# Scores from stacked split queries over 128 rows, in a given TensorE order between projection pieces

## The chip, the cores and the metric

The kernel runs on one core of one Trainium2 chip. The metric is the device time of one execution in microseconds (us). A core has a matrix engine (TensorE, PE in the profile), a vector engine (VectorE, DVE), a scalar engine for activations and copies (ScalarE, ACT), a general engine (GpSimd, POOL) and SyncE (SP), which issues transfers; DMAs can also be issued from ACT's queue. The engines run beside each other and wait for one another by semaphores. On-chip memory is SBUF, and TensorE writes its sums to PSUM.

## What is computed

Two layers of a decoder on 512 tokens of 1024 channels, in float32. Layer 0 is attention, layer 1 is RWKV-7; each is followed by a squared-ReLU MLP of width 4096. The change lies in layer 0:

```python
def hybrid_attention(h, w_in, w_out, lam_p, subln, lam_init):
    proj = h @ w_in
    aq, ak, av, bq, bk, bv = jnp.split(proj, cuts, axis=-1)      # 512 columns each
    aq = partial_rope(heads(aq, A_HEADS), pos) * scale           # 8 heads of 64
    ak = partial_rope(heads(ak, A_HEADS), pos)
    oa = mixture_of_dilations(aq, ak, heads(av, A_HEADS))        # mixer A
    ...
    bq = partial_rope(two_maps(bq), pos) * scale                 # 4 heads, 2 maps of 64
    bk = partial_rope(two_maps(bk), pos)
    lam = jnp.exp(jnp.sum(lp[0] * lp[1])) - jnp.exp(jnp.sum(lp[2] * lp[3])) + lam_init
    ob = differential_attention(bq, bk, heads(bv, B_HEADS), lam, subln, lam_init)
    return jnp.concatenate([oa, ob], axis=-1) @ w_out
```

Mixer A mixes three causal, dilated windows by their softmax denominators, which is one softmax with the logarithm of how often each key occurs added to its score. Mixer B is `(softmax(s0) - lam * softmax(s1)) @ v` for two maps of each head, then an RMS norm over the head's 128 outputs.

## The kernel before

**Products.** A product with a weight matrix is made in three single-pass products (type float32r) of parts that have been split into a high and a low part: high by high, high by low, low by high (`mm3`, lines 174 to 178). `wchunk` loads two blocks of 128 weight rows by 512 columns (`wraw`, from SP), ACT casts the high part (`whi`), VectorE subtracts for the low part (`wlo`). `gemm_group` runs a product over four PSUM banks: for each chunk of two blocks, four banks `m` by two blocks `k`, three products each. Activations are split in the same way (`xh`, `xl`; `oh`, `ol` for the attention's outputs; `split`).

**Attention.** The order in the code is: values `va`, queries `qa`, keys `ka`, mixer A (`attend_a`), then `qb`, `kb`, `vb`, then mixer B (`attend_b`), then the output product with `Wo` (two halves of 512 input rows, two column groups), whose evacuation adds to the residual `h`. `project_qk` evacuates each block of 128 channels so: ACT copies it (`qraw`), VectorE multiplies it by the cosine, four DMAs on ACT's queue swap the rotated channels (`sw`), POOL multiplies these by the sine (`rt`), and VectorE adds. Queries use tables with the factor -0.125 in them (`cosq`, `sinq`).

Scores are one float32 product over the 64 rows of a head, 128 queries by `n` keys (`n` is 128, 256, 384 or 512 by query block `i`; the trace shows two instructions for each). Two heads (mixer A) or two maps (mixer B) lie in the two halves of the 128 rows. `probs` then adds the mask table and finds the row minimum on VectorE (`sb`, `mn`), and ACT makes the exp with its row sum. `pv` transposes the result on TensorE (`t`), ACT copies it (`pts`), TensorE multiplies it by the values (`o`). `attend_a` goes over query blocks, in each over eight heads; `attend_b` over query blocks, in each over four heads and two maps, with `w` and the subtraction of the maps on VectorE, then squares (`junk`), a power on POOL (`rs2`) and the scaled output `ob`. `to_channels` transposes an `ob` on TensorE and splits it into `oh`, `ol`.

**Order.** The code's order is not the engines' order: a scheduler in the build places instructions of different steps by its own reckoning, under dependences and free buffers. In attention nothing else fixes the order but a few dependences between value products. So projections of mixer B and the first half of `Wo` fall between steps of the mixers where the scheduler put them. In the RWKV layer the class `InOrder` ties instructions of an engine into the order in which they are written.

Of the kernel before, what the change touches and what calls it, by code (L numbers as in the profile page):

```python
# [10 lines left out]
F32 = mybir.dt.float32  # L11
# [7 lines left out]
P = 128  # L19
S = 512  # L20
# [89 lines left out]
""".split())  # L110
HU = 4
CW = HU * HD

# [31 lines left out]
class Builder:  # L145
# [67 lines left out]


    def build(self):
        tc, nc, A = self.tc, self.nc, self.A
        with ExitStack() as ctx:
# [3 lines left out]
            self.const = pool("const")  # L221
            self.open_w()
# [29 lines left out]
            self.open_h()  # L252

# [9 lines left out]
            self.close_w()  # L263

# [95 lines left out]
    def attention_layer(self):  # L360
        tc, nc, A = self.tc, self.nc, self.A
        with ExitStack() as ctx:
# [10 lines left out]
            cosq, sinq = (ac.tile([P, S], F32, name=n) for n in ("cosq", "sinq"))  # L373
            dl = ac.tile([P, 4 * HD], F32, name="dl")
            sub = ac.tile([P, 1], F32, name="sub")

# [35 lines left out]
            def project_v(c0, name, meanwhile=None, prep=None):  # L412
# [4 lines left out]
                self.gemm_group(W, 0, KT, c0, xh, xl, evac, token_major=True, meanwhile=meanwhile, prep=prep, chunk=prep and chunk)  # L417
                return v
            for k in range(AHEAD):
                channels(k)  # L420
            va = project_v(1024, "a", token_norm, lambda k: k + AHEAD < KT and channels(k + AHEAD))
            xin.release()
            aw = pool("aw", 2)
            prb = self.bcast(r0)
            for t, tq in ((cos, cosq), (sin, sinq)):
                nc.vector.tensor_tensor(t, t, prb, op=ALU.mult)
                nc.gpsimd.tensor_scalar(tq, t, -0.125, None, op0=ALU.mult)
# [6 lines left out]
            def project_qk(c0, name, ct, st):  # L434
                q = ac.tile([P, NB, S], F32, tag="Q" + name, name=self.nm("Q" + name))

                def evac(m, ps):
# [4 lines left out]
                    nc.vector.tensor_tensor(q[:, m, :], ps, ct, op=ALU.mult)  # L442
# [4 lines left out]
                    nc.gpsimd.tensor_tensor(t, sw, st, op=ALU.mult)  # L447
                    nc.vector.tensor_tensor(q[:, m, :], q[:, m, :], t, op=ALU.add)
                self.gemm_group(W, 0, KT, c0, xh, xl, evac)
                return q  # L450

            def probs(q, k, mm_, hh, i, table, total):
# [3 lines left out]
                rows = slice(hh * HD, (hh + 1) * HD)  # L456
                ps = ps_s.tile([P, S], F32, tag="s", name=self.nm("s"))
                nc.tensor.matmul(ps[:, :n], q[rows, mm_, i * P:(i + 1) * P], k[rows, mm_, :n], start=True, stop=True)
# [1128 lines left out]
```

## Time and profile before

| | |
|---|---|
| time, median of 3 runs | 1525.69 us (1523.87 to 1530.07) |
| profiled execution | 1525.81 us, of which its span is 1523.9 |
| TensorE busy | 1443.8 us, 95% |
| VectorE, ACT, POOL busy | 57%, 45%, 23% |
| mean granted TensorE clock | 0.976 of full speed |
| attention from the end of `ka` to the first MLP product | 88.9 to 294.2 us |

The span is the time from the first to the last instruction. A share of busy time is a mean over stages with different limits. TensorE's instructions overlap: one starts before the one ahead of it has ended, so what a product costs is read from one start to the next, not from its own length.

### The profile page before, as it was taken

The page shows a single profiled execution, that of the slowest core. Times are in us where ns is not written, and L with a number is a line of the kernel's source. Part 1 is how long each engine was busy: PE and PEld are TensorE (multiplying, and loading weights), DVE is VectorE, ACT ScalarE, POOL GpSimd, SP SyncE. Part 2 cuts the span into 40 slices and gives each one's busy share as a digit, 9 for nine tenths or more (in the row PEclk, how much of TensorE's full clock was granted, in tenths as well). Part 3 has the DMA queues.
Part 4 walks back from the last instruction along what each step waited for, and adds up shares of the span by engine and source line. Part 5 has one row for each costly group of instructions (what it writes and reads, how often), then busy time and mean ns, then how long its engine had stood idle before and what let it go on. Part 6 is the DMA issues. An engine that isn't in the chain of part 4 may idle for free. (4 is left out here: it accounts for less than half of the span.)

```text
span 1523.9 us, 24386 instructions
## 1 busy us (share of the span) xinstructions
PE 1443.8 (95%) x9506; PEld 1172.4 (77%) x9506; DVE 863.7 (57%) x1491; ACT 684.2 (45%) x1394; POOL 352.0 (23%) x364
## 2 busy tenths in 40 slices
PE   7999999999999999969888999989998999999998
PEld 6765866878888888857667788868787888888887
DVE  5343565632335464497876778878866333354543
ACT  4245364432334343236634666666655233343533
POOL 4210200300000010052336455546655000000100
PEclk9999999999999999979989999989999999999999
DMA  5230310433333233324564345444223333333331
GB/s 193 80 90 1 96 57 27 102 104 85 97 97 97 97 124 98 102 64 152 176 192 147 116 139 154 127 143 119 64 95 118 90 97 97 97 97 97 97 97 70
DMA packets 117115, 159.76 MB, mean 105 GB/s; under 512 B 22524, under 2 KB 57892, under 8 KB 117000
## 3 DMA queue, kind: packets, MB, share of 16 engines
q1 hardware_dynamic: 103240, 140.37, 30.8%
q10 hardware_dynamic: 13760, 17.83, 3.5%
q8 instruction: 75, 1.23, 0.3%
q14 instruction: 40, 0.33, 0.1%
HBM read 133.00 MB, written 19.92 MB: 100 GB/s over the span
## 5 line engine op out<-in xcount | busy, mean ns | idle before, releaser
L169 DVE TENSOR_TENSOR wlo<-wraw,whi 128x1024 fp32r<-128x1024 f32 x172 | 219.9, 1280 | 263.1 <-ACT whi L167 263.0
L167 ACT CAST whi<-wraw 128x1024 fp32r<-128x1024 f32 x172 | 180.5, 1050 | 253.0 <-PE g L177 236.2
L176 PE MATMUL g<-xh,whi 128*128 128x512 f32 x640 | 250.2, 391 | 1.1 <-DVE Qa L442 1.1
L178 PE MATMUL g<-xh,wlo 128*128 128x512 f32 x640 | 249.0, 391 | 1.3 <-DVE wlo L169 1.1
L177 PE MATMUL g<-xl,whi 128*128 128x512 f32 x640 | 249.8, 390 | 0.0
L176 PE MATMUL g<-mh,whi 128*128 128x512 f32 x512 | 199.2, 389 | 0.0
L177 PE MATMUL g<-ml,whi 128*128 128x512 f32 x512 | 199.2, 389 | 0.0
L178 PE MATMUL g<-mh,wlo 128*128 128x512 f32 x512 | 199.2, 389 | 0.0
L316 POOL TENSOR_TENSOR acc<-acc,sq 128x512 f32<-128x512 f32 x29 | 48.8, 1683 | 636.4 <-issue 436.5
L184 DVE TENSOR_TENSOR ml<-m,mh 128x512 fp32r<-128x512 f32 x128 | 90.0, 706 | 148.9 <-ACT mh L183 148.8
L183 ACT CAST mh<-m 128x512 fp32r<-128x512 f32 x128 | 78.7, 616 | 191.3 <-PE g L178 191.1
L178 PEld LDWEIGHTS g<-xh,wlo 128*128 128x128 f32 x640 | 120.1, 188 | 28.3 <-DVE wlo L169 3.0
L176 PEld LDWEIGHTS g<-xh,whi 128*128 128x128 f32 x640 | 120.1, 188 | 27.2 <-DVE Qa L442 1.8
L177 PEld LDWEIGHTS g<-xl,whi 128*128 128x128 f32 x640 | 120.3, 188 | 24.7 <-issue 0.3
L178 PEld LDWEIGHTS g<-mh,wlo 128*128 128x128 f32 x512 | 96.1, 188 | 20.1
L176 PEld LDWEIGHTS g<-mh,whi 128*128 128x128 f32 x512 | 96.1, 188 | 20.1
L177 PEld LDWEIGHTS g<-ml,whi 128*128 128x128 f32 x512 | 96.1, 188 | 19.7
L137 POOL TENSOR_TENSOR wlo<-wraw,whi 128x256 fp32r<-128x256 f32 x100 | 76.6, 770 | 119.3 <-ACT whi L137 115.3
L177 PE MATMUL g<-wlo,xh 128*128 128x512 f32 x160 | 65.3, 408 | 4.5 <-DVE wlo L169 4.5
L176 PE MATMUL g<-whi,xh 128*128 128x512 f32 x160 | 63.0, 408 | 5.8 <-ACT xh L641 4.7
L643 POOL TENSOR_TENSOR xl<-mt,xh 128x512 fp32r<-128x512 f32 x28 | 47.5, 1712 | 86.9 <-ACT xh L641 73.5
L178 PE MATMUL g<-whi,xl 128*128 128x512 f32 x160 | 65.0, 406 | 0.6 <-POOL xl L643 0.5
(313 smaller groups left out, 2757.8 us busy)
## 6 DMA issues: line engine op xcount, KB each, us to landing
wraw<-in_mlp_w_dram SPq DMA_DIRECT2D x128, 512.0 KB
wraw<-in_attn_w_in_dram SPq DMA_DIRECT2D x24, 512.0 KB
wraw<-in_rwkv_w_o_dram SPq DMA_DIRECT2D x16, 512.0 KB
wraw<-in_attn_w_out_dram SPq DMA_DIRECT2D x8, 512.0 KB
wraw<-in_rwkv_w_k_dram SPq DMA_DIRECT2D x8, 512.0 KB
wraw<-in_rwkv_w_r_dram SPq DMA_DIRECT2D x8, 512.0 KB
wraw<-in_rwkv_w_v_dram SPq DMA_DIRECT2D x8, 512.0 KB
xt<-in_x_dram ACTq DMA_DIRECT2D x4, 512.0 KB
```

What stands on the lines that cost most here:

```text
L137: ins = op(*args, **kw)
L167: ins = [nc.scalar.copy(hi, raw)]
L169: ins.append((eng or nc.vector).tensor_tensor(lo, raw, hi, op=ALU.subtract))
L176: mm(ps, lh, rh, start=start, stop=False)
L177: mm(ps, lh, rl, start=False, stop=False)
L178: mm(ps, ll, rh, start=False, stop=stop)
L183: nc.scalar.copy(hi, src)
L184: nc.vector.tensor_tensor(lo, src, hi, op=ALU.subtract)
L316: nc.gpsimd.tensor_tensor(self.acc[0], self.acc[0], sq, op=ALU.add)
L643: eng.tensor_tensor(xl[k], t, xh[k], op=ALU.subtract)
```

## The change

- **Scores.** `stacked` puts the high part of a head's scaled query in its own 64 rows and the low part in the other 64 (type float32r); the key's high part (`kh`) and low part (`kl`) are each copied by a DMA into the other half, so that they stand twice. A score is then two single-pass products over 128 rows, with `kh` and with `kl`, which make all four products of the parts. `cosq` and `sinq` go; the factor -0.125 is in `stacked`.
- **By head pairs.** Mixer A runs over four pairs of heads, in each over two heads and four query blocks (8 slots); mixer B over four heads, in each over four query blocks (4 slots) with both maps. Outputs are normed and turned into channels by pair or head, and `Wo` runs in three parts (rows 0 to 3, 4 to 5, 6 to 7).
- **In a given order.** `at` gives each step a slot: in mixer A a score at slot + 0.6, its transposes at + 1.3, its value product at + 2.0; in mixer B at + 0.6, + 2.2 and + 2.8. `gemm_stream` gives the products of `qb`, `kb`, `vb` and `Wo` in 160 pieces of three products, and `FILL` says how many pieces are issued by which slot. `InOrder` fixes the order on TensorE alone; the other engines keep the scheduler's.
- **Buffers.** `sb` has 6 buffers instead of 4, `ob` 2 instead of 5. Six `fill` tiles of 64 to 224 bytes are written once and never read.

```diff
+FILL = [(-2, 0), (-1, 0), (0, 18), (33, 96), (36, 104), (48, 140), (60, 144)]
...
+            self.edge = self.tc.alloc_tile_pool(name="edge", bufs=1, side="right")
+            self.fill(self.edge, 224)
...
+    def fill(self, pool, size):
+        self.nc.gpsimd.memset(pool.tile([P, size // 4], F32, tag="fill", name=self.nm("fill"), bufs=1), 0.0)
...
+            def stacked(q, k):
+                maps = []
+                for hh in range(2):
+                    own, other = SIDES[hh], SIDES[1 - hh]
+                    qs, kh, kl = (aw.tile([P, S], F32R, tag=f"{n}{hh}", name=self.nm(n)) for n in ("qs", "kh", "kl"))
+                    nc.scalar.activation(qs[own], q[own], AF.Copy, scale=-0.125)
+                    nc.vector.scalar_tensor_tensor(qs[other], q[own], -0.125, qs[own], op0=ALU.mult, op1=ALU.subtract)
+                    nc.scalar.copy(kh[own], k[own])
+                    nc.scalar.dma_start(kh[other].bitcast(F32), kh[own].bitcast(F32))
+                    nc.vector.tensor_tensor(kl[own], k[own], kh[own], op=ALU.subtract)
+                    nc.scalar.dma_start(kl[other].bitcast(F32), kl[own].bitcast(F32))
+                    maps.append((qs, kh, kl))
+                return maps
...
-                nc.tensor.matmul(ps[:, :n], q[rows, mm_, i * P:(i + 1) * P], k[rows, mm_, :n], start=True, stop=True)
-                sb = aw.tile([P, S], F32, tag="sb", name=self.nm("sb"), bufs=4)
+                nc.tensor.matmul(ps[:, :n], qs[:, i * P:(i + 1) * P], kh[:, :n], start=True, stop=False)
+                nc.tensor.matmul(ps[:, :n], qs[:, i * P:(i + 1) * P], kl[:, :n], start=False, stop=True)
...
+                sb = aw.tile([P, S], F32, tag="sb", name=self.nm("sb"), bufs=6)
...
+            plain, nc = nc, InOrder(self, ["tensor"])
...
+            pieces, emitted = self.gemm_stream(jobs), 0
...
+            for slot, _, f in sorted(events, key=lambda e: e[:2]):
+                want = np.interp(slot, *zip(*marks))
+                while emitted < want:
+                    next(pieces)
+                    emitted += 1
+                f()
+            for _ in pieces:
+                pass
```

What that makes of the engines' orders stands in the two built programs. On TensorE, in mixer A at scores of 384 keys, before (`t` transposes, `s` scores, `o` value products):

```order
L458 MATMUL s_990<-Qka_579,Qa_414 128x384
L477 MATMUL o_845<-Va_210,pts_916 64x64 x4
L471 MATMUL t_928<-ident,sb_924 128x128 x2
L458 MATMUL s_1008<-Qka_579,Qa_414 128x384
L477 MATMUL o_845<-Va_210,pts_931 64x64 x4
L471 MATMUL t_943<-ident,sb_939 128x128 x2
```

And now (`g` are products of the `kb` projection):

```order
L149 MATMUL s_1106<-kh_797,qs_796 128x384
L149 MATMUL s_1106<-kl_798,qs_796 128x384
L149 MATMUL g_1090<-xh_151,whi_934 128x512
L149 MATMUL g_1090<-xl_159,whi_934 128x512
L149 MATMUL g_1090<-xh_151,wlo_936 128x512
L149 MATMUL o_921<-Va_219,pts_1101 64x64 x4
L149 MATMUL g_1090<-xh_152,whi_934 128x512
L149 MATMUL g_1090<-xl_160,whi_934 128x512
L149 MATMUL g_1090<-xh_152,wlo_936 128x512
L149 MATMUL t_1123<-ident,sb_1109 128x128 x3
```

Three projection products now stand between one step of the mixer and the next, where before the steps of neighbouring heads stood in a row.

On ACT, where the `kb` projection's blocks are evacuated, before:

```order
L167 CAST whi_1640<-wraw_1638 128x1024
L441 COPY qraw_1575<-g_1469 128x512
L444 DMA sw_408<-qraw_1575 8x512
L445 DMA sw_408<-qraw_1575 8x512
...
L441 COPY qraw_1591<-g_1470 128x512
L167 CAST whi_1670<-wraw_1668 128x1024
L444 DMA sw_409<-qraw_1591 8x512
L445 DMA sw_409<-qraw_1591 8x512
```

And now (the same pair of DMAs follows once more where lines are left out):

```order
L537 ACTIVATE sb_1417,sums_1413<-sb_1417,mn_1418 128x128
L516 DMA kl_1563<-kl_1563 64x512
L546 COPY pts_1437<-t_1435 128x128
L492 COPY qraw_1442<-g_1090 128x512
L495 DMA sw_418<-qraw_1442 8x512
L496 DMA sw_418<-qraw_1442 8x512
...
L537 ACTIVATE sb_1455,sums_1413<-sb_1455,mn_1456 128x256
L492 COPY qraw_1468<-g_1091 128x512
L546 COPY pts_1481<-t_1478 128x256
```

Exps of mixer A (`sb`, `sums`) now stand between the evacuations, one to each.

On TensorE, where the last outputs of mixer B are turned into channels, before (`g_2283` the transposes, the rest `Wo`):

```order
L177 MATMUL g_2291<-ol_1764,whi_2326 128x512
L486 MATMUL g_2283<-ident,ob_2281 128x128 x4
L178 MATMUL g_2291<-oh_1762,wlo_2328 128x512
L176 MATMUL g_2291<-oh_1762,whi_2326 128x512
L177 MATMUL g_2291<-ol_1764,whi_2326 128x512
```

And now (`oc` the transposes):

```order
L149 MATMUL t_2701<-ident,sb_2668 128x128 x4
L149 MATMUL o_2644<-Vb_778,pts_2706 128x128 x4
L149 MATMUL g_2639<-oh_1916,whi_2497 128x512
L149 MATMUL g_2639<-ol_1920,whi_2497 128x512
L149 MATMUL g_2639<-oh_1916,wlo_2499 128x512
L149 MATMUL oc_2735<-ident,ob_2729 128x128 x4
L149 MATMUL g_2640<-oh_1915,whi_2497 128x512
```

Three products of `Wo` now stand between the last value product and the last output transposes; before, 13 did, and as the lines show others stand right behind the transposes.

## Rows read from the trace of the kernel before

**Rows 1.** The page: busy time of TensorE, and the chain that ended last.

```profile
PE 1443.8 (95%) x9506; PEld 1172.4 (77%) x9506; DVE 863.7 (57%) x1491; ACT 684.2 (45%) x1394; POOL 352.0 (23%) x364
...
PE g L178 8%; PE g L177 8%; PE g L176 8%; PE g L1368 0%; PE g L1551 0%; PE g L342 0%; DVE wlo L169 0%; DVE xl L187 0%; DVE h L1413 0%; POOL wlo L1363 0%; DVE yc L137 0%; ACT xh L186 0%; POOL yc L137 0%; ACT o L1558 0%; PE g L356 0%; PE tf L137 0%
```

**Rows 2.** Busy time by stretch: us, engines (instructions), granted clock, DMA share, GB/s.

```profile
88.90:294.20 205.30, 198.55 (x1147) 138.98 (x1147) 110.49 (x278) 101.30 (x262) 26.49 (x20) 0.99 0.18 55
...
294.20:560.00 265.80, 264.10 (x1171) 218.56 (x1170) 112.25 (x130) 93.56 (x127) 8.50 (x7) 1.00 0.34 98
```

**Rows 3.** The same by stretch, the score tiles' instructions alone (PE, PEld, DVE).

```profile
88.90:156.00 67.10, 22.41 (x64) 7.69 (x64) 15.47 (x32) 1.00 0.10 28
156.00:294.20 138.20, 19.57 (x64) 7.46 (x64) 15.30 (x32) 0.99 0.22 69
```

**Rows 4.** Timeline of TensorE (start, length), in the MLP and at 256-column products.

```profile
419.70 0.39 PE L178 MATMUL g<-xh,wlo 128*128 128x512 f32 x1
419.93 0.39 PE L176 MATMUL g<-xh,whi 128*128 128x512 f32 x1
...
861.78 0.28 PE L137 MATMUL side<-whi,xh 128*128 128x256 f32 x1
861.90 0.28 PE L137 MATMUL side<-wlo,xh 128*128 128x256 f32 x1
```

**Rows 5.** Timeline of TensorE in mixer A, scores of 256 and of 512 keys.

```profile
109.13 0.70 PE L458 MATMUL s<-Qka,Qa 64*128 64x256 f32 x4
109.76 0.45 PE L477 MATMUL o<-Va,pts 128*64 128x64 f32 x8
...
110.51 0.70 PE L458 MATMUL s<-Qka,Qa 64*128 64x256 f32 x2
111.13 0.50 PE L176 MATMUL g<-xh,whi 128*128 128x512 f32 x1
...
128.22 1.12 PE L458 MATMUL s<-Qka,Qa 64*128 64x512 f32 x2
129.27 0.57 PE L477 MATMUL o<-Va,pts 128*64 128x64 f32 x12
```

**Rows 6.** Timeline of TensorE, projection products behind a block of transposes.

```profile
146.78 0.65 PE L471 MATMUL t<-ident,sb 128*128 128x128 f32 x4
147.19 0.48 PE L177 MATMUL g<-xl,whi 128*128 128x512 f32 x1
147.51 0.40 PE L178 MATMUL g<-xh,wlo 128*128 128x512 f32 x1
```

**Rows 7.** Timeline of ACT and its DMA issues (ACTq), `ka` evacuations and exps.

```profile
85.25 0.59 ACT L441 COPY qraw<-g 128x512 f32<-128x512 f32 x1 [2.83 <-DMA sw<-qraw]
85.73 1.06 ACT L167 CAST whi<-wraw 128x1024 fp32r<-128x1024 f32 x1
85.92 0.63 ACTq L444 DMA_DIRECT2D sw<-qraw  x1
86.58 0.63 ACTq L445 DMA_DIRECT2D sw<-qraw  x1
...
88.67 0.59 ACT L441 COPY qraw<-g 128x512 f32<-128x512 f32 x1 [1.89 <-DMA sw<-qraw]
...
97.03 0.41 ACT L464 ACTIVATE sb<-sb,mn 128x128 f32<-128x128 f32 x1 [2.59 <-DMA sw<-qraw]
...
97.44 0.39 ACT L464 ACTIVATE sb<-sb,mn 128x128 f32<-128x128 f32 x1
```

**Rows 8.** Groups by line and shape, 88.9 to 294.2 us: busy us, mean ns.

```profile
L464 ACT ACTIVATION_READ_ACCUMULATOR sb<-sb,mn 128x1 f32 x64 | 12.2, 191 | 0.0
L464 ACT ACTIVATE sb<-sb,mn 128x512 f32<-128x512 f32 x16 | 11.6, 726 | 3.2 <-DVE mn L461 2.9 <-DVE w L518 0.2
...
L169 DVE TENSOR_TENSOR wlo<-wraw,whi 128x1024 fp32r<-128x1024 f32 x19 | 25.3, 1334 | 23.6 <-ACT whi L167 23.5
L461 DVE CUSTOM_DVE_ANT_0 sb<-s,logc 128x512 f32<-128x512 f32 x8 | 5.5, 692 | 9.0 <-PE t L471 9.0
```

**Rows 9.** Timeline at the last outputs of mixer B: squares, output, transposes.

```profile
251.20 0.28 ACT L525 ACTIVATE junk<-o 128x128 f32<-128x128 f32 x1 [1.31 <-PE o L477]
...
255.06 0.66 PE L486 MATMUL g<-ident,ob 128*128 128x128 f32 x4 [0.95 <-DVE ob L535]
```

**Rows 10.** Busy time by stretch of 2 us, as in rows 2, with the granted clock.

```profile
220.00:222.00 2.00, 2.00 (x13) 1.91 (x11) 1.82 (x7) 1.28 (x3) 0.00 (x0) 0.55 0.00 0
222.00:224.00 2.00, 2.00 (x6) 0.75 (x5) 0.94 (x5) 1.08 (x3) 0.00 (x0) 0.59 0.00 0
```

More of the change, by code (lines that the diff above doesn't have):

```diff
@@ L252, in build @@
             self.open_h()
+            self.fill(c, 64)
+            self.fill(self.tmp, 128)
             self.attention_layer()
@@ L476, in pv @@
                     for o in range(0, P, rows):
-                        ins = nc.tensor.matmul(po[o:o + rows, col:col + width], pts[:, j * P + o:j * P + o + rows],
-                                               v[:, j, col:col + width], start=(j == 0), stop=(j == i))
-                        if j == 0 and o == 0 and prev is not None:
-                            self.after(ins, prev)
-                return ins
-            def to_channels(ob, hi, lo, i, scale=None):
-                pt = self.bank()
-                for t in range(4):
-                    nc.tensor.transpose(out=pt[:, t * P:(t + 1) * P], in_=ob[:, t * P:(t + 1) * P], identity=self.ident)
-                qs = slice(i * P, (i + 1) * P)
-                self.split(pt.rearrange("p (t q) -> p t q", q=P), hi[:, :, qs], lo[:, :, qs], scale)
@@ new lines, in attention_layer, with at, steps_a, prepare @@
+            events, prepared, oh_ready = [], {}, set()
+            def at(slot, f):
+                events.append((slot, len(events), f))
+            def steps_a(q, k, v, oh, ol, slot0):
+                for m in range(4):
+                    u = {}
+                    def prepare(m=m):
+                        prepared["a", m] = stacked(q[m], k[m])
+                    first = slot0 + 8 * m
+                    at(first - 4 if m else slot0 - 1, prepare)
+                    for hh in range(2):
+                        for i in range(NB):
+                            t, w = first + 4 * hh + i, {}
+                            def score(m=m, hh=hh, i=i, u=u, w=w):
+                                if "sums" not in u:
+                                    u["sums"] = sm.tile([P, NB, 2], F32, tag="sums", name=self.nm("sums"), bufs=2)
+                                w["p"] = probs(scores(prepared["a", m][hh], i), i, logc, u["sums"][:, i, hh:hh + 1])
+                            def turn(i=i, w=w):
+                                w["t"] = turned(w["p"], i)
+                            def values(m=m, hh=hh, i=i, u=u, w=w):
+                                if "po" not in u:
+                                    u["po"] = ps_o.tile([P, S], F32, tag="o", name=self.nm("o"))
+                                pv(w["t"], i, v, m * P + hh * HD, i * P + hh * HD, HD, u["po"])
+                                if hh and i == NB - 1:
+                                    normed_a(u)
+                            at(t + 2.0, values)
+                            at(t + 1.3, turn)
+                            at(t + 0.6, score)
+                    def channels(m=m, u=u):
+                        to_channels(u["ob"], oh[m], ol[m])
+                        oh_ready.add(m)
+                    at(first + 10.4, channels)
@@ L569, in attention_layer @@
[L569 to L576 removed]
+            (qb, job_qb), (kb, job_kb), (vb, job_vb) = project_qk(1536, "b"), project_qk(2048, "kb"), project_v(2560, "b")
```

229 lines of the change are left out of this document (151 added, 78 removed).

## The prediction

> **What bounds the kernel now.** I read the page first: TensorE is busy 95% of the span, and the chain that ended last runs over the lines of the split projections [rows 1]. Then the order of both programs: on TensorE the first 301 rows and the last 8,158 are the same work in the same order, so the change acts between the end of the `ka` projection (88.9 us) and the first MLP product (294.2 us), a stretch of 205.3 us. In it TensorE is busy 198.6 us and idle 6.7; in the MLP behind it 264.1 of 265.8 [rows 2]. So before, nearly everything in the stretch is TensorE time, and the MLP passes on any shift of its start in full. Two questions decide: how much TensorE time goes, and how much waiting comes in.
>
> The profiled execution took 1525.81 us against a median of 1525.69, so what is worked out on the trace is added to the median as it stands.
>
> **Scores: −21.9 us.** The 64 scores hold TensorE 22.4 us in mixer A and 19.6 in mixer B, 42.0 together [rows 3]. After, each is two single-pass products over 128 rows. A product of 512 columns of that type starts 0.227 us after the one ahead and one of 256 columns 0.12 [rows 4]; 384 lies between, 0.173, and for 128 columns I take 0.107 (no row has it; half of the 256 would be 0.06). Sixteen scores of each length, two products each: 32 × (0.227 + 0.173 + 0.12 + 0.107) = 20.1 us. The lower end (0.06) is 18.6; the upper end, a 0.1 us switch at each score, is 26.5.
>
> There is something against stacking at all. Two scores of the two row halves already run side by side: four instructions of 256 columns take 0.63 us to the next start, two take 0.62 [rows 5]. The Trainium skill ("TensorE: Matmul & The Clock Gate", Part 3: Packing small matmuls) says that matmuls in different row groups run at once, and the trace agrees. By that rule alone mixer B, whose two maps stand together, would halve its scores by pairing them; the sum of [rows 3] already holds what pairs there were.
>
> **Everything else on TensorE: about +5 us.** Projections, transposes, value products and output transposes are the same in number, but the score, turn and value steps now alternate with projection pieces, where before mixer A ran mostly transpose, score, value in a row (the first order excerpt). The first projection product behind a block of transposes takes 0.32 us to the next start instead of 0.227 [rows 6]: a change of kind costs about 0.09. Counted in the two orders over the stretch, TensorE goes from one kind of work to another 173 times before and 272 after, +99, or 8.9 us. But 83 of these are between projection products and stacked scores, now of one type and shape of weights; if they cost nothing, it is 1.4. I take +5, ends 0 and 10.
>
> **ACT's DMA issues in mixer A: about +13 us.** This is the term I trust most. Each rotated block of a q or k projection is copied out (`qraw`) and swapped by four DMAs issued on ACT's queue, and an issue holds that queue: they start 0.665 us apart, and the next `qraw` comes 3.42 us after the one ahead, with a 1.05 us cast hidden beneath [rows 7]. Before, `qb` and `kb` are evacuated while TensorE does only projections. After, both bursts of four stand between the exps of mixer A on ACT's queue, and TensorE, whose order is fixed, waits for the exp at its next transposes. ACT's time from one exp to another, by rows 7 and 8 (an exp starts 0.41 us after the one ahead at 128 columns, though it and its read last 0.40 and 0.19; so I take 0.18 off each exp and 0.1 off each copy):
> - First burst: 16 issues at 0.665 = 10.6, and the exps, copies and casts that don't lie beneath them 8.7, together 19.3 us. TensorE's work from the score behind the first of these exps to the transposes that need the last is 14 projection pieces (of three products, 9.5 us), scores 1.6, transposes 1.6, values 2.2: 14.9. It waits 4.4.
> - Second burst: 18 issues (two are the duplicated k halves) = 12.0, the rest 8.4, together 20.4. TensorE's work there is 10 pieces (6.8), scores 1.3, transposes and output transposes 2.1, values 1.8: 12.0. It waits 8.4.
> Outside the bursts ACT has room: the two casts of `stacked` for each map (like a copy, 0.6 to 0.7) included, a pair without a burst takes it 16 to 19 us, where TensorE has 22 to 25 of work.
>
> **Other waits: about 9 us, against 6.7 before.** The start: `stacked` of the first pair needs the roped k, a cast, a DMA and a subtract, but 18 pieces (12.2 us) stand ahead of the first score: 0.5. Other slots in A: score to transpose is a reduction of at most 0.69, the exp of 0.73 + 0.19 and their hand-overs, 1.2 to 1.9 us [rows 8], against 1.0 to 2.0 us of TensorE work in between: some 0.1 each, 3 us. Mixer B: the longest chain (two reductions, two exps, weight, subtraction) is 3.4 us and has 1.6 slots, about 6 us, of cover; 2 us for order on VectorE, where the `stacked` subtracts, the h additions and `wlo` (1.34 [rows 8]) queue. The end: from the last score TensorE has 3.9 us of work until the last transposes, which are ready at 3.4; it then waits for their copy (0.9) and, after the last values and one piece, for the norm of the last head. Before, the squares began at 251.20 and the output transposes at 255.06, 3.86 us later, and TensorE covered this with projection products [rows 9]; now one piece (0.7) stands there and the values have just ended: 3.4 us of wait, and sixteen pieces remain that all hang on it or follow it. Sum 0.5 + 3 + 2 + 0.9 + 3.4 = 9.8. A half-clock stretch after that wait would cost what the one after 218 to 220 us did, four microseconds at 0.55 to 0.59 of full speed, 1.7 us [rows 10]; before has it too, so nothing is added.
>
> POOL loses two small scalings and gains six small fills ahead of the work; SP's queue is unchanged in order. The 32 duplicating DMAs move 128 KB each while the 16 engines are 18% busy [rows 2]; only their issue counts, and it is in the ACT sums (those outside the bursts lie under slack).
>
> **The sum.** −21.9 + 5 + 12.8 + 9.8 − 6.7 = −1.0: 1525.7 − 1.0, near **1525 us**. Its ends: scores −23.4 to −15.5, switching 0 to 10, burst waits 6 to 18, other waits −1 to +9 against before. All low would be −18, all high +21; together I hold 1513 to 1538.
>
> **Rivals.**
> 1. *The memory offsets.* The six fills have no reader; they move tiles. In the built program before, every operand of a single-pass product starts 32 bytes past a multiple of 64; after, at multiples of 256. Those products start 0.227 us apart for 512 columns, and 512 columns at 2.4 GHz (granted 1.00 [rows 2]) are 0.2133: 13 ns more, and 13 more at 256 columns (0.12 against 0.107) too [rows 4]. If 11 of the 13 hang on the offset, 4,280 + 960 such products gain 58 us. RWKV's 16-bit tiles go the other way (multiples of 64 to 32 past), some 1,400 products by the same 11 to 13 ns at most, −18: net 40 to 58, say 52: 1473. For it: the excess is the same at either length, as a fixed price per product is. Against it: it may as well be a price of changing weights; the score at 128.22, its operands at the same offset, takes 1.05 us, which is four passes of 512 columns (0.853) and two weight loads of 0.1 [rows 5], and no row has an aligned product. The Trainium skill ("TensorE: Matmul & The Clock Gate", Wait — 56ns, not 53.3ns?) measured 215.7 ns back to back at 512 columns; by that page all 11 ns could go, though it does not say what operands it used, and the trace's 227 differs.
> 2. *ACT stalls on the duplicated halves* (the slower side). A duplicating DMA of `kl` stands on ACT's queue and waits there for VectorE's subtract; exps queue behind it, and TensorE waits for these. It decides if VectorE is later than ACT, which happens where a 1.34 us `wlo` or two reductions lie ahead of the subtract [rows 8]. 32 such DMAs, 16 of them `kl`; about 1 us each at 16 places: 1525 + 15 = 1540.
> 3. *The bursts are covered.* If pieces and values of other slots fill the bursts (the upper switching cost is work under which ACT catches up), 13 us of wait shrink to 3 and the saving stays: about 1513.
>
> That the scores don't become cheaper is hardly possible: two passes replace four, and the order shows them.
>
> **How the numbers follow.** Forecast 0.40, offsets 0.34, ACT stalls 0.14, covered 0.12. A measurement of this kernel tells about 0.5%, 7.6 us, from no change: faster is below 1518, slower above 1533. Faster: nearly all of the offsets' case, 0.10 of the covered one, 0.04 of the forecast's low end: 0.47. Slower: 0.13 of the stalls, 0.05 of the forecast's high end: 0.18. Same: 0.35. The range, 1462 to 1537, leaves out the offsets' extreme and most of the stalls; without the offsets it would be 1513 to 1538.
>
> **What would show it.** Right: the first MLP product near 293 us; two TensorE gaps summing to 4 to 9 us each, ended by ACT's exp, at about 105 to 120 and 148 to 170 us, with `qraw` DMA issues beneath; a gap of 3 to 4 us ended by `ob` near 280. Wrong: projection products 0.216 apart everywhere (offsets); exps late behind `kl` issues (stalls); score products dearer than 0.23 at 512 columns.

## The result, and the profile after

| | before | after |
|---|---|---|
| time, median of 6 runs | 1525.37 us (1523.84 to 1530.07) | 1539.2 us (1535.18 to 1544.92) |
| ratio, 95% interval | | 1.0088 (1.0062 to 1.0114) |
| profiled execution, its span | 1525.81, 1523.9 us | 1535.18, 1533.4 us |
| first MLP product | 294.2 us | 304.1 us |

The change makes the kernel 0.9% slower; the forecast was 1525 us and the range ended at 1537. The profiled execution after is the shortest of its six, so its sums explain 9.4 of the 13.8 us between the medians. The other five have mean granted clocks of 0.965 to 0.973, where this one has 0.977, and the longest has the lowest: the rest goes with more time at the half clock, and no trace shows where in the program that lies.

The page of after, the line that answers to [rows 1]:

```profile
PE 1429.2 (93%) x9506; PEld 1176.0 (77%) x9506; DVE 893.1 (58%) x1531; ACT 702.4 (46%) x1426; POOL 348.4 (23%) x368
```

TensorE has 14.6 us less busy time and the program is longer all the same: it waits. Busy time by stretch (us, then engines with instructions, granted clock, DMA share, GB/s), answering to [rows 2]; the last row is the rest of the program:

```profile
88.90:304.10 215.20, 184.72 (x1146) 142.66 (x1144) 129.25 (x310) 115.69 (x286) 23.96 (x18) 0.97 0.25 69
...
304.10:1533.00 1228.90, 1164.44 (x8013) 968.62 (x8011) 713.98 (x1153) 553.78 (x1096) 297.21 (x320) 0.98 0.37 111
```

In attention 30.5 us are not busy, against 6.7 before; from the MLP's start to the end the two executions differ by less than half a microsecond (1229.7 before, 1229.3 after). So the whole difference lies ahead of 304.1. Shorter stretches of after, in the same columns, show where:

```profile
88.90:103.00 14.10, 11.72 (x45) 9.17 (x44) 6.01 (x8) 4.44 (x6) 4.19 (x3) 0.88 0.33 83
103.00:128.00 25.00, 18.57 (x128) 13.54 (x127) 13.07 (x27) 11.42 (x28) 4.71 (x4) 1.00 0.31 79
128.00:153.00 25.00, 24.41 (x182) 17.82 (x181) 11.08 (x27) 13.20 (x31) 1.21 (x1) 1.00 0.33 90
153.00:178.00 25.00, 18.07 (x123) 12.86 (x122) 13.36 (x25) 12.65 (x27) 5.15 (x4) 0.93 0.24 62
178.00:203.00 25.00, 24.03 (x179) 17.55 (x178) 11.84 (x28) 13.32 (x31) 0.00 (x0) 1.00 0.24 71
...
240.00:260.00 20.00, 16.88 (x90) 14.11 (x88) 15.43 (x46) 11.28 (x35) 1.01 (x1) 0.92 0.29 79
```

The rows at 103 and 153 are the two bursts in which ACT evacuates `qb` and `kb` and issues their DMAs; between them TensorE is full. The table of TensorE's waits in this stretch (line waited, instruction waited for: us in total, times, longest):

```profile
PE t L149 <- ACT sb L537: 9.7, 11, 2.5
PE o L149 <- ACT pts L546: 6.8, 7, 2.0
PE g L149 <- DVE Qka L493: 4.3, 2, 2.4
PE o L149 <- ACT sb L537: 3.8, 2, 2.2
PE oc L149 <- DVE ob L592: 3.3, 1, 3.3
PE o L149 <- DVE w L658: 2.6, 1, 2.6
...
```

Added up by place, from the last product of `ka` (it starts at 88.20 us before and 2.7 us earlier, at 85.48, after) to the MLP, the same 1,149 TensorE rows in both, and with the time from each TensorE start to the next put down to the first of the two, less any wait between them:

| us | before | after | difference |
|---|---|---|---|
| scores | 39.0 | 22.1 | −16.9 |
| all other work on TensorE | 160.2 | 164.1 | +3.8 |
| waits | 6.75 | 32.4 | +25.7 |
| sum | 206.0 | 218.6 | +12.6 |

The +3.8 is the clock: 13.65 us of after's stretch lie at the lower level, against 3.4 before, and 10.2 us at half speed cost 5.1. Without that the other work takes 1.3 us less.

### The profile page after: what moved, and what is told of

The parts are those of the page before. It is cut to its first block, busy times and chain, and to the rows that moved or that the text cites. A ratio compares the mean times of both kernels' runs of the same rounds, so it can differ in the third digit from the quotient of the medians.

```text
span 1533.4 us, 24513 instructions
## 1 busy us (share of the span) xinstructions
PE 1429.2 (93%) x9506; PEld 1176.0 (77%) x9506; DVE 893.1 (58%) x1531; ACT 702.4 (46%) x1426; POOL 348.4 (23%) x368
## 5 line engine op out<-in xcount | busy, mean ns | idle before, releaser
L190 PE MATMUL g<-xh,wlo 128*128 128x512 f32 x576 | 224.1, 390 | 1.1 <-DVE wlo L181 1.0
L188 PE MATMUL g<-xh,whi 128*128 128x512 f32 x576 | 225.0, 391 | 0.1
L189 PE MATMUL g<-xl,whi 128*128 128x512 f32 x576 | 224.6, 390 | 0.0
L190 PEld LDWEIGHTS g<-xh,wlo 128*128 128x128 f32 x576 | 108.2, 188 | 24.7 <-DVE wlo L181 2.4
L188 PEld LDWEIGHTS g<-xh,whi 128*128 128x128 f32 x576 | 108.2, 188 | 23.4 <-DVE Qa L493 0.6
L189 PEld LDWEIGHTS g<-xl,whi 128*128 128x128 f32 x576 | 108.2, 188 | 21.9
L149 POOL TENSOR_TENSOR wlo<-wraw,whi 128x256 fp32r<-128x256 f32 x100 | 76.5, 768 | 121.6 <-ACT whi L149 117.9
L149 PE MATMUL side<-whi,xh 128*128 128x256 f32 x192 | 63.6, 331 | 0.0
L188 PE MATMUL g<-whi,xh 128*128 128x512 f32 x128 | 51.3, 415 | 5.4 <-ACT xh L802 4.7
L1673 DVE TENSOR_TENSOR m<-m 128x512 f32<-128x512 f32 x64 | 44.1, 689 | 20.0 <-ACT m L1672 20.0
```

Source lines behind the costliest of these rows:

```text
L149: ins = op(*args, **kw)
L188: mm(ps, lh, rh, start=start, stop=False)
L189: mm(ps, lh, rl, start=False, stop=False)
L190: mm(ps, ll, rh, start=False, stop=stop)
L1673: nc.vector.tensor_tensor(t, t, t, op=ALU.mult)
```

## Experiments

Each ratio is to the kernel before, with its 95% interval. First came single parts of the waits (e1, e2), the offsets (e3) and the scores (e4).

**e1: the swap DMAs off ACT's queue.**

```diff
+                    issuer = nc.sync if name in ("b", "kb") else nc.scalar
-                        nc.scalar.dma_start(sw[o:o + 8], raw[o + 8:o + 16])
+                        issuer.dma_start(sw[o:o + 8], raw[o + 8:o + 16])
```

> The changed kernel with one edit: the four swap DMAs of each block of qb and kb are issued on SP's queue instead of ACT's (those of qa and ka stay). Theory (ACT's DMA issues hold the exps that TensorE waits for): the waits of the changed kernel at 111 to 127 us (6.4 us) and at 161 to 177 us (6.9 us) go, and with them the half-clock stretch at 161 us: 11 to 15 us less than the changed kernel's 1539, 1524 to 1528 us. Rival (ACT is short of time there in any case, by its casts, exps and copies, or the stacked operands are late): the waits stay or come back a few slots later, 1535 to 1540 us.

Measured: 1532.46 us, ratio 1.0054 (1.0035 to 1.0073). About half of what was expected. In after, the second burst looks like this (start, length, engine, in brackets the idle time ahead and what ended it):

```profile
163.21 0.59 ACT L492 COPY qraw<-g 128x512 f32<-128x512 f32 x1 [1.01 <-PE g L149]
163.87 0.64 ACTq L495 DMA_DIRECT2D sw<-qraw  x1
164.55 0.64 ACTq L496 DMA_DIRECT2D sw<-qraw  x1
165.23 0.63 ACTq L495 DMA_DIRECT2D sw<-qraw  x1
165.90 0.63 ACTq L496 DMA_DIRECT2D sw<-qraw  x1
166.58 0.51 ACT L537 ACTIVATE sb<-sb,mn 128x256 f32<-128x256 f32 x1 [2.78 <-DMA sw<-qraw]
...
167.24 0.44 PE L149 MATMUL t<-ident,sb 128*128 128x128 f32 x2 [1.20 <-ACT sb L537]
```

Four issues hold ACT for 2.8 us, the exp starts when the last has gone, and TensorE waits for the exp. With the issues on SP's queue the waits of both bursts fall from 13.3 to 6.9 us. What is left goes another way, seen in e1 at the same place:

```profile
163.73 0.62 SPq L497 DMA_DIRECT2D sw<-qraw  x1
...
165.20 3.39 POOL L499 TENSOR_TENSOR rt<-sw,sin 128x512 f32<-128x512 f32 x2 [2.81 <-DMA sw<-qraw]
...
167.38 1.76 DVE L500 TENSOR_TENSOR Qkb<-Qkb,rt 128x512 f32<-128x512 f32 x1 [1.18 <-POOL rt L499]
...
169.66 0.67 DVE L535 CUSTOM_DVE_ANT_0 sb<-s,logc 128x512 f32<-128x512 f32 x1
...
170.38 0.72 ACT L538 ACTIVATE sb<-sb,mn 128x512 f32<-128x512 f32 x1 [2.10 <-DVE mn L535]
...
171.25 0.44 PE L149 MATMUL t<-ident,sb 128*128 128x128 f32 x2 [2.74 <-ACT sb L538]
```

On VectorE the mask and minimum of the next score (169.66) stand behind the addition of the rotated block, and that waits for POOL, which waits for the swaps. The rotation still ends in a queue that the mixer needs, VectorE's instead of ACT's.

**e2: the value bank freed by a copy.** At a border between heads in mixer B the one bank of `o` must wait until `ob` has read it.

```diff
                 po, sums = u["po"], u["sums"]
+                held = aw.tile([P, S], F32, tag="held", name=self.nm("held"), bufs=1)
+                nc.scalar.copy(held, po)
+                po = held
```

> The changed kernel with one edit: in mixer B, ACT copies a head's value products from their PSUM bank into SBUF before the norm, and the norm works on the copy, so that the one bank comes free 0.6 us after the last value product instead of after the whole norm. Theory (the waits of 2.2, 2.6 and 1.5 us before the first value product of heads 1 to 3 are for that bank): these 6.3 us and the half-clock stretch at 240 us go, the last norm gets 0.5 us longer: 4 to 8 us less than 1539, 1531 to 1535 us. Rival (they are waits for the exps and the weight w, as the profile names them): no change, 1537 to 1541 us.

Measured: 1537.9 us, 1.0087 (1.0067 to 1.0107): no gain. The waits for the bank go, and the next steps in the order wait for the same norm in their place: a score, for the bank in which the head's output was turned into channels (`oc` and `s` share two), and a piece of `Wo`, for these channels. The last wait grows from 3.33 to 4.02 us. Timeline of TensorE in e2, the two largest of the new ones:

```profile
248.84 0.38 PE L149 MATMUL s<-kh,qs 128*128 128x128 f32 x1 [1.78 <-DVE ol L199]
...
266.05 0.51 PE L149 MATMUL g<-oh,whi 128*128 128x512 f32 x1 [1.40 <-ACT oh L198]
```

**e3: without the six fills**, so that the tiles stand where they would without them.

```diff
-        self.nc.gpsimd.memset(pool.tile([P, size // 4], F32, tag="fill", name=self.nm("fill"), bufs=1), 0.0)
+        return
```

> The changed kernel without the six fill tiles, so that all tiles stand at other SBUF offsets. Theory (offsets do nothing; single-pass products start 0.227 us apart in the trace of the changed kernel as in the one before): the changed kernel's time, 1536 to 1542 us, products 0.227 us apart. Rival (the offsets cost or save time somewhere): 5 us or more to either side, with another spacing of some product.

Measured: 1541.09 us, 1.0106 (1.0083 to 1.0130), as after. Single-pass products start 0.227 us apart in e3, as they do in after and before.

**e4: the old scores in the given order.** Stacking is undone: one float32 product over a head's 64 rows, with neither the casts nor the duplicating DMAs.

```diff
-                nc.tensor.matmul(ps[:, :n], qs[:, i * P:(i + 1) * P], kh[:, :n], start=True, stop=False)
-                nc.tensor.matmul(ps[:, :n], qs[:, i * P:(i + 1) * P], kl[:, :n], start=False, stop=True)
+                nc.tensor.matmul(ps[:, :n], qs[rows, i * P:(i + 1) * P], k[rows, :n], start=True, stop=True)
```

> The changed kernel with the score products of before: float32 over the 64 rows of a head, the query scaled by one VectorE operation for a pair; no split halves, no duplicating DMAs. Steps, slots and pieces as in the changed kernel. Theory (the stacked scores save 17 us of TensorE time, and their casts and DMAs cost little where they stand): slower than the changed kernel by 8 to 17 us, since part of the longer scores covers waits: 1547 to 1556 us. Rival (stacking is what costs, by 32 DMA issues and 32 casts on ACT): no slower than the changed kernel, 1530 to 1540 us.

Measured: 1552.1 us, 1.0189 (1.0162 to 1.0216), 12.9 us more than after. So stacking saves time, and whatever loses it is in the rest of the change.

**e5 and e6: the rotation's addition on POOL too.** e5 is e1 with this line; e6 issues the swaps of `qa` and `ka` from SP as well.

```diff
-                    nc.vector.tensor_tensor(q[m], q[m], t, op=ALU.add)
+                    (nc.gpsimd if name in ("b", "kb") else nc.vector).tensor_tensor(q[m], q[m], t, op=ALU.add)
```

> The swaps of qb and kb on SP as in e1, and the addition that ends the rotation of qb and kb on POOL instead of VectorE. In e1 part of the second burst came back as waits of 1.5 and 2.7 us (at 165.6 and 171.3 us): there the score's reduction stood behind that addition on VectorE, which waited for POOL's product, which waited for the swap DMAs. Theory (the same chain now holds VectorE's queue instead of ACT's): those waits go, 1532.5 falls by 3 to 5 us to 1527 to 1530. Rival (VectorE is late there by its other work): no change, 1531 to 1534 us.

> As e5, with the swap DMAs of qa and ka on SP too. In the changed kernel the first pieces of qb wait 1.96 and 2.38 us for the banks of ka, which VectorE and ACT evacuate one block in 3.4 us, since four DMA issues stand between two copies on ACT's queue; a half-clock stretch follows. Theory (the same hold of ACT's queue): these 4.3 us and the stretch go, 4 to 6 us below e5, 1521 to 1526 us, which is the time of the kernel before or a little less. Rival (the weight loads on SP's queue now come late behind the swap DMAs, or the banks wait for VectorE): no better than e5.

Measured: e5 1527.31 us, 1.0016 (1.0003 to 1.0029); e6 1525.46, 0.9994 (0.9977 to 1.0011). In e5's profiled execution the waits of both bursts are 4.0 us, against 6.9 in e1 and 13.3 in after: VectorE's queue was a good part of what e1 left, and not all of it. In e6's profiled execution the MLP starts at 288.9 us, 5.3 earlier than before, but the program behind takes 1236.0 us, 6.3 more: the half-clock stretches past 310 us add up to 76.5 us there and to 64.9 before.

**e7: the kernel before with its swaps of `qb` and `kb` on SP's queue**, the edit of e1 in the old kernel.

```diff
+                    issuer = nc.sync if name in ("b", "kb") else nc.scalar
-                        nc.scalar.dma_start(sw[o:o + 8], raw[o + 8:o + 16])
+                        issuer.dma_start(sw[o:o + 8], raw[o + 8:o + 16])
```

> The kernel before with the swap DMAs of qb and kb on SP. Theory (before, these bursts stand while TensorE does projections alone and nothing waits for ACT): no change, 1522 to 1528 us. Rival (moving these DMAs helps any kernel, and e1 says nothing of the change): 4 us or more faster, under 1521 us.

Measured: 1538.46 us, 1.0088 (1.0065 to 1.0112). Neither theory has this. The row of the stretch in which it is lost (columns as above):

```profile
209.00:237.00 28.00, 26.81 (x75) 16.22 (x75) 14.94 (x72) 13.06 (x52) 1.04 (x1) 0.51 0.07 20
```

TensorE is busy nearly throughout and its clock is granted at 0.51: one stretch of 27.3 us (209.3 to 236.6) at the lower of the two levels, where the kernel before has 0.94 over the same window. It begins behind a wait of 1.81 us that ends at 208.02 and within one of 0.92 that ends at 209.64. Half speed over 27.3 us costs 13.7, which is 12.0 more than the 3.4 us at the lower level cost the kernel before there; from the last `ka` product to the MLP the run takes 12.5 us longer, and its median is 13.7 longer (1538.46 against 1524.81 beside it). On the DMA issues this run decides nothing. It does show that a program can lie 12 us off by the clock alone.

**e8: later pieces.** More of `Wo` is kept for the last slots, to cover the last norm.

```diff
-FILL = [(-2, 0), (-1, 0), (0, 18), (33, 96), (36, 104), (48, 140), (60, 144)]
+FILL = [(-2, 0), (-1, 0), (0, 18), (33, 96), (36, 104), (48, 132), (52, 144), (60, 144)]
```

> The changed kernel with eight pieces fewer up to slot 48 and six instead of one between the last value product and the last output transposes. Theory (there TensorE waits 3.3 us for the last norm, with nothing else to do, and a half-clock stretch follows): that wait goes, but the waits for the one bank at the heads' borders grow by about 0.5 us each, since less work covers the norms there: 2 to 4 us less than 1539, 1535 to 1537 us. Rival (what is won at the end is lost in full at the borders): 1538 to 1541 us.

Measured: 1540.1 us, 1.0108 (1.0091 to 1.0125), as the rival had it: the end wait shrank from 3.33 to 0.32 us, and the waits at the borders went from 2.24, 2.55 and 1.51 to 3.25, 2.46 and 3.77. Pieces moved from one hole open another.

**e9 and e10: the borders, and everything together.** e9 has e2's copy, the channels one and a third slots later, and pieces spread by head; e10 is e9 with e6's edits.

```diff
-FILL = [(-2, 0), (-1, 0), (0, 18), (33, 96), (36, 104), (48, 140), (60, 144)]
+FILL = [(-2, 0), (-1, 0), (0, 18), (33, 96), (45.2, 126), (53, 142), (60, 144)]
...
-                    at(first + 7.9, channels)
+                    at(first + 9.2, channels)
```

> The changed kernel with e2's copy of the value products, and with mixer B's output transposes at slot + 9.2 instead of + 7.9 and the pieces of Wo spread so that no step waits for a norm that has just begun: (33, 96), (45.2, 126), (53, 142), (60, 144). In e2 the waits of 2.2, 2.6 and 1.5 us at the heads' borders went, but 1.8, 1.4 and 0.9 us came at the next steps that need the same norm. Theory (a head's norm, 3.9 us from squares to output, has too little work behind it in any form): now they go, and the wait of 3.3 us at the end too: 6 to 10 us below the changed kernel's 1539, 1529 to 1533 us. Rival (mixer B is bound by VectorE, and a wait taken away comes back elsewhere): 1536 to 1541 us.

> e6 (swap DMAs on SP, the rotation's addition on POOL) and e9 together. Theory (the two groups of waits are independent): e6's 1525.5 less what e9 wins, 1516 to 1520 us, faster than the kernel before by 0.3 to 0.6%. Rival (TensorE's half-clock stretches in the RWKV layer, which no edit touches and which cost e6 some 6 us there, take back what attention wins): 1521 to 1526 us.

Measured: e9 1533.66 us, 1.0044 (1.0021 to 1.0067), just past its expectation's end; e10 1516.67, 0.9942 (0.9922 to 0.9961), as expected. Waits in attention are 23.4 us in e9 and 15.8 in e10. With the waits mended one by one, the change gains at last. The row of e10's attention has TensorE's work unchanged and the clock whole:

```profile
82.00:282.50 200.50, 184.71 (x1171) 142.60 (x1170) 131.13 (x306) 120.56 (x295) 37.87 (x27) 1.00 0.29 81
```

**e11: no given order.** The same steps, written in the same sequence, but TensorE is left to the scheduler.

```diff
-            plain, nc = nc, InOrder(self, ["tensor"])
+            plain, nc = nc, nc
```

> The changed kernel without the given order: the same steps written in the same sequence, but the scheduler in the build places TensorE's instructions as it did in the kernel before. Theory (the change lost its gain by the given order, which puts both evacuation bursts and the heads' norms in front of TensorE): several us less waiting, 1528 to 1535 us. Rival (the waits come from ACT's and VectorE's queues and from the sequence of steps, not from TensorE's order): 1536 to 1545 us.

Measured: 1510.63 us, 0.9898 (0.9872 to 0.9925), better than expected, and 28.6 us less than after with ACT's DMA issues where they were. Its attention, from the end of `ka` to the MLP:

```profile
85.50:273.60 188.10, 181.00 (x1153) 141.02 (x1152) 128.19 (x311) 112.87 (x286) 20.20 (x17) 0.99 0.29 83
```

The waits are 7.1 us. Why, shows at the first burst. ACT in e11, its copies out of projections and its exps there:

```profile
115.25 0.52 ACT L537 ACTIVATE sb<-sb,mn 128x256 f32<-128x256 f32 x1
...
118.27 0.60 ACT L492 COPY qraw<-g 128x512 f32<-128x512 f32 x1
...
121.62 0.37 ACT L546 COPY pts<-t 128x256 f32<-128x256 f32 x1 [1.81 <-POOL rt L498]
121.89 0.62 ACT L537 ACTIVATE sb<-sb,mn 128x384 f32<-128x384 f32 x1
```

No exp starts between 115.25 and 121.89: ACT is held as in after's bursts. And TensorE in the same time, first and last rows of a run of 17 projection products:

```profile
119.85 0.44 PE L544 MATMUL t<-ident,sb 128*128 128x128 f32 x2
120.05 0.49 PE L188 MATMUL g<-xh,whi 128*128 128x512 f32 x1
...
123.90 0.39 PE L189 MATMUL g<-xl,whi 128*128 128x512 f32 x1
124.22 0.45 PE L553 MATMUL o<-Va,pts 128*64 128x64 f32 x8
```

After's order puts two or three pieces (six to nine products) in a slot of mixer A whatever ACT does; here a whole run of them stands where ACT is held, and fewer stand later.

**e12: the given order with more pieces at the bursts.**

```diff
-FILL = [(-2, 0), (-1, 0), (0, 18), (33, 96), (36, 104), (48, 140), (60, 144)]
+FILL = [(-2, 0), (-1, 0), (0, 18), (3, 25), (7, 43), (16, 57), (20, 79), (33, 96), (36, 104), (48, 140), (60, 144)]
```

> The changed kernel with one table changed: pieces of qb and kb are not spread evenly over mixer A's slots but put where ACT evacuates a block: (0, 18), (3, 25), (7, 43), (16, 57), (20, 79), (33, 96) instead of (0, 18), (33, 96). Eight more pieces, 5.4 us, stand in slots 3 to 7, and some twelve more, 8 us, in slots 16 to 20; the slots between get fewer. Theory (the order is not bad for being given but for being even: TensorE meets exps at an even pace that ACT can't keep during its DMA issues): the two groups of 6.4 and 6.9 us of waits shrink to about 4 in sum, small waits of 0.2 us appear in the thin slots: 1528 to 1533 us. Rival (the given order loses by something else that the scheduler's order avoids): 1536 to 1541 us.

Measured: 1541.08 us, 1.0108 (1.0093 to 1.0123), as the rival had it. The burst waits fell from 13.3 to 8.9 us, but the thinner slots got waits of up to 1.91, and the sum stayed (32.9 us); 30.7 us of its attention lie at the half clock, against 13.65 in after. ACT's order, which is the scheduler's, came out differently as well, with two evacuations and no exp between. So this run doesn't show that the even spread alone is to blame.

**e13 and e14: e11 with the DMA issues moved, and e11 with the old scores.** e13 is e11 with e6's edits, e14 is e11 with e4's.

> e11 (TensorE's order left to the scheduler) with e6's edits (swap DMAs on SP, the rotation's addition on POOL). Theory (where TensorE has projection products to do during the bursts, the hold of ACT's queue costs nothing): no change against e11, 1507 to 1513 us. Rival (the hold costs in any order): 4 to 12 us below e11, 1499 to 1506 us.

> e11 with the score products of before (as e4: float32 over 64 rows, no stacking). Theory (the stacked scores are worth 17 us of TensorE time, and with few waits they show in full): e11 + 12 to 18 us, 1523 to 1529 us, about the kernel before. Rival (what e11 wins it wins by the steps' sequence by head pairs, not by the scores): 1508 to 1516 us.

Measured: e13 1509.91 us, 0.9901 (0.9887 to 0.9916), the same as e11; e14 1523.41, 0.9984 (0.9970 to 0.9998). The first says that ACT's DMA issues cost nothing measurable where the scheduler places TensorE's work around them, though the same edits were worth 14 us in the given order (after to e6). The second completes a table of four:

| median, us | given order | scheduler's order |
|---|---|---|
| old scores | 1552.1 (e4) | 1523.41 (e14) |
| stacked scores | 1539.2 (after) | 1510.63 (e11) |
| difference | −12.9 | −12.8 |

Across, the order costs 28.7 us with the old scores and 28.6 with the stacked ones. The four were not all run beside each other; by their ratios to the kernel before, stacking saves 15 and 13 us and the order costs 31 and 29, which agree within the intervals (0.3 to 0.5% of 1525 us wide, 4 to 8 us). So the two parts of the change add up, each with its own sign: stacking is worth some 13 us, and the fixed order costs some 29.

The traces show what the order's price consists of, here with the old scores, e4 and then e14 (columns as above; what TensorE's busy time leaves of a stretch is waiting):

```profile
86.00:316.70 230.70, 208.20 (x1151) 135.05 (x1150) 114.62 (x290) 101.83 (x260) 24.65 (x19) 0.98 0.16 48
...
87.10:291.30 204.20, 199.17 (x1151) 133.54 (x1150) 113.10 (x288) 97.91 (x258) 20.60 (x17) 1.00 0.17 56
```

Waits are 22.5 us with the order and 5.0 without; with the stacked scores they are 32.4 (after) and 7.1 (e11). In either row of the table the order also brings 10.2 us more at the half clock, worth 5.1. So from `ka` to the MLP it costs 26.6 us with the old scores and 30.9 with the stacked ones. Behind the MLP's start the two runs without it are 5 and 8 us longer, with 13 and 19 us more at the half clock, in a part of the program that no edit touches; that both rows of the table come to 29 is in part chance.

The old scores by head pairs in the scheduler's order (e14) take about what the kernel before takes: what is left of the change without its order and its scores, the new loops above all, is worth some 2 us (0.3 to 4.6 by the interval).

## Why the prediction was wrong

The saving and the waits at the bursts and the end were foreseen. Three steps failed: what the first pieces of `qb` wait for, what the heads' borders wait for, and what a wait costs in clock. By the terms of the sum, in us:

| term | predicted | measured in after |
|---|---|---|
| scores | −21.9 | −16.9 |
| other TensorE work, switching | +5 | −1.3 |
| ACT's two bursts | 4.4 + 8.4 | 6.4 + 6.9 |
| start | 0.5 | 4.3 |
| other slots | 3 | 3.8 |
| heads' borders in B | 2 | 6.3 |
| end | 0.9 + 3.4 | 1.35 + 3.3 |
| waits of before | −6.7 | −6.75 |
| clock | 0 | +5.1 |
| sum | −1.0 | +12.6 |

The sum was off by 13.6 us. Start, borders and clock were put at 0.5, 2 and 0 and came to 15.8, which makes 13.3 of it; the other errors nearly cancel.

**Right: the bursts and the end.** The term that the prediction trusted most came to 13.3 against 12.8, partly by luck: the first burst was 2.0 over its price and the second 1.5 under. They stand at 111 to 127 and 161 to 177 us, 6 to 13 us later than said. For 8.0 us they are ended by ACT's exps, as said, and for 5.2 by its copies of the transposes, with the `qraw` issues ahead of them; e1 took half of them away by moving the issues. The end is there to a few tenths:

```profile
287.72 1.01 POOL L400 TENSOR_TENSOR rs<-ss,expo 128x4 f32<-128x4 f32 x1 [12.90 <-DVE ss L588]
...
289.70 0.66 PE L149 MATMUL oc<-ident,ob 128*128 128x128 f32 x4 [3.33 <-DVE ob L592]
```

**Wrong by 5: the scores.** 42.0 us were read as busy time [rows 3], and busy times overlap. From start to start the old scores hold TensorE 39.0. That is 3 of the 5; the other 2 are the new products, 22.1 instead of 20.1. The same view as [rows 3] shows how far it misleads, after:

```profile
88.90:200.00 111.10, 14.03 (x56) 10.29 (x56) 13.04 (x28) 0.97 0.29 77
200.00:304.10 104.10, 15.66 (x72) 12.78 (x72) 17.42 (x37) 0.97 0.22 59
```

29.7 us busy, 22.1 from start to start.

**Wrong by 6.3 the other way: switching.** A change of kind was read as 0.09 us [rows 6], times 99. After has those changes, and outside the half clock its other work takes no longer than before. In e4, with the old scores among the same steps, that work takes 8.8 us more than in after, counted in the same way: this fits a change of kind that has a price beside the old scores and none beside the stacked ones, the case for which the prediction worked out 1.4. The errors on scores and switching nearly cancelled, by luck.

**Wrong by 3.8: the start.** The prediction looked at the first score and not at the pieces ahead of it. The first `qb` pieces need the four banks that `ka` still holds, and each is freed only when ACT and VectorE have taken a block out. Between two blocks stand ACT's four DMA issues, 3.42 us apart in [rows 7] and here about 4:

```profile
87.09 0.68 DVE L493 TENSOR_TENSOR Qka<-g,cos 128x512 f32<-128x512 f32 x1
...
87.83 0.50 PE L149 MATMUL g<-xh,whi 128*128 128x512 f32 x1 [1.96 <-DVE Qka L493]
...
91.87 0.50 PE L149 MATMUL g<-xh,whi 128*128 128x512 f32 x1 [2.38 <-DVE Qka L493]
```

e6, with these issues on SP, still waits 1.67 and 1.47 us; e11, where the scheduler placed other work there, 0.6 for a bank.

**Wrong by 4.3: the heads' borders.** The chain that was priced for mixer B (reductions, exps, weight) is not what TensorE waited for: e2 leaves it as it is, and these waits go. What was missed is a resource: `o` of mixer B has one bank, and the next head's first value product can't start until the whole norm of the head before has read it. After, at the first border:

```profile
236.56 1.01 POOL L400 TENSOR_TENSOR rs<-ss,expo 128x4 f32<-128x4 f32 x1 [58.97 <-DVE ss L588]
...
238.16 0.68 DVE L592 TENSOR_TENSOR ob<-o,rs 128x512 f32<-128x512 f32 x1
...
238.99 0.46 PE L149 MATMUL o<-Vb,pts 128*128 128x128 f32 x2 [2.24 <-ACT sb L537]
```

The row names ACT's exp, but the product starts 0.15 us after `ob` ends. The three borders are 2.24, 2.55 and 1.51 us. The same norm was costed correctly at the end of mixer B and forgotten three times ahead of it. e2 shows that a second copy alone doesn't help, since the order makes the next steps wait for the same norm; e9, which moves those steps as well, gains.

**Wrong by 5.1: the clock.** "Nothing is added" was the step. After has four stretches of 3.4 us at the lower level in attention (from 93.1, 161.4, 239.9 and 291.1 us), each within 1.5 us of the end of a wait of 2.2 to 3.3 us; before has one. The clock in the rows above, 0.88, 0.93 and 0.92, is theirs. Four waits in the given order were thus paid 1.7 us dearer each, and 5.1 is what that is above before's one. This was in reach: [rows 10] were quoted with that price, for one.

**The rest.** `ka` ends 2.7 us earlier in after's profiled execution (1.7 of it is a half-clock stretch at 15.4 us that this execution of before had), so the MLP starts 9.9 us later and not 12.6.

**The rivals.** The offsets, which widened the range down to 1462, are out: after, TensorE in the MLP,

```profile
429.80 0.39 PE L188 MATMUL g<-xh,whi 128*128 128x512 f32 x1
430.02 0.39 PE L189 MATMUL g<-xl,whi 128*128 128x512 f32 x1
```

with operands at multiples of 256 bytes, as the prediction read the built program, start 0.227 us apart (430.25 the next), as in [rows 4] and in e3. The Trainium skill ("TensorE: Matmul & The Clock Gate", Wait — 56ns, not 53.3ns?) has 215.7 ns for this length; no run here reaches it with this type, so 0.227 stands. The stall on duplicated halves gave the right side and time, 1540 us, for the wrong reason: in after no issue of `kl` on ACT starts more than 0.15 us behind what stands ahead of it in the queue, so ACT did not wait for VectorE's subtract, and the losses stand at other places. That the bursts are covered is what happens in e11, not in the given order.

**What the list of terms hides.** The forecast costed each wait by the work beside it, and got the bursts, the end and the other slots. It didn't ask what kind of thing it was costing: a change that saves 13 us on TensorE and pays 29 for a fixed order on TensorE, while ACT and VectorE keep an order of the scheduler's making. The table of four shows this price, and e13 that a hold on ACT costs nothing measurable where the scheduler placed TensorE's work. That it does so because TensorE has other work there is read from the one burst shown in e11, and not tested.

**What stays open.** Which feature of the order costs the most: e12 changed the spread of the pieces and ACT's order with it, so the even spread was not tried alone. And the half-clock stretches behind the MLP's start, 55 to 77 us in the profiled executions with no edit there: e11's profiled execution starts its MLP 20.6 us earlier than before's and ends only 13.2 earlier (76.6 us at the half clock past 310, against 64.9). In attention they run from none (e10, e14) to 30.7 us (e12). What moves them was not tested, and the time of each run includes them.

## What to carry to other kernels

An order fixed on one engine is only as good as the times at which the others deliver; leave it to the scheduler, or (not tried here) fix it on all that take part, and when you cost it walk each queue and each PSUM bank along the whole order, not only at its ends. Read what an instruction costs from its start to the next start, since busy sums overlap (42.0 against 39.0 us, and 29.7 against 22.1). And test a change of two parts as a table of four before you trust the sum: here a gain of 13 us was hidden under a loss of 29, and the change without its order (1510.63 us, or 1509.91 with e6's edits) beats the kernel before by 1.0% and the changed one by 1.9%.

## What the runs showed of the hardware

- **The price of a wait.** Waits of 2.24 to 3.33 us on TensorE were followed by a 3.4 us stretch at the lower clock, 1.7 us of time, in four places of after; in e7 waits of 1.81 and 0.92 us came with 27.3 us of it, in which TensorE was busy nearly throughout. Not every such wait has one: that of 2.55 us at the second border of after, which ends at 258.80, has none, and e10 has waits up to 1.7 us and none in attention.
- **DMA issues hold the queue of the engine that makes them.** Four of them take ACT 2.8 us (163.87 to 166.58), computing nothing behind them. SP's take as long (0.62), but nothing that the mixer needs queues there.
- **Offsets don't matter here.** Single-pass products of 512 columns start 0.227 us apart in before and in after, with operands 32 bytes past a multiple of 64 and at multiples of 256 as the prediction read the two built programs.
